# Rows on POOL's queue, one route for both tiles, and the second norm's scale and shift by feature, in a two-layer trunk

## The chip, the cores and the metric

The kernel runs on one core of a Trainium2 chip. The metric is the device time of one execution in microseconds; the kernel before takes 2118.0 us, the median of three runs (2116.41 to 2120.69). PE is the matmul engine, DVE, ACT and POOL are the vector, scalar and GpSimd engines, and SP issues most of the transfers.

## The reference

Two layers act on 256 latent and 256 context rows of 1024 features; layer 1 updates the latent rows alone. A layer normalizes and modulates its rows, projects them, mixes them in three branches (Hyena, gated DeltaNet or GDN, latent attention), merges these under gates, and projects with `w_out`. Then comes a second norm and a mixture of 16 experts, two for each row. What the change touches is this:

```python
def gdn_output(o, z, lp):
    on = o * lax.rsqrt(jnp.mean(o * o, axis=-1, keepdims=True) + EPS) * lp['gdn_norm_g']
    y = on * jax.nn.silu(z).reshape(B, L, H, DV)
    return y.reshape(B, L, H * DV) @ lp['gdn_out']

# in a layer; mix is the merged branches times w_out
x = x + gt1 * mix
h2 = rms_norm(x, lp['norm2_g']) * (1.0 + sc2) + sh2
x = x + gt2 * moe_ffn(h2, router_w, router_b, lp)

def moe_ffn(h, router_w, router_b, lp):
    scores = jax.nn.sigmoid(h @ router_w)
    sel = scores + router_b
    # the group of four experts with the largest sum of its two best, then the two best in it
    ...
    for e in range(N_EXPERTS):
        he = jax.nn.silu(h @ lp['moe_w1'][e]) * (h @ lp['moe_w3'][e])
        out = out + gate[:, e:e + 1] * (he @ lp['moe_w2'][e])
```

## The kernel before, in words

Rows are held in tiles of 128: four in layer 0 (two of x, two of ctx), two in layer 1. SBUF is an arena of 47 pages of 128x1024 floats, handed out and taken back as the program goes; `M.get(2)` takes one page. The program is written out by a planner: each piece of work is an item with loads, a preparation, matmuls and a post, and generators (`start`, with a `yield` wherever another piece may be put in) run beside the items. The planner keeps an estimated clock for each engine and queue (`enter`, lines 225 to 320, where a gather counts 2500 ns beyond its transfer) and with it decides what is written next; after that every engine works through its own instructions in the order written. Every operation goes through one helper, so all rows of the profile show line 210, and tiles are told apart by their names.

`wout_items` (line 1772) makes the output projection. An item takes a block of 128 rows of `w_out`, which ACT and DVE split into a high and a low part (the CAST is ACT's, the subtraction DVE's), and then three matmuls for each half of each tile. Layer 0 has two groups of two tiles, layer 1 one group. At item `ROWK` (0 in layer 0, 2 in layer 1) it calls `rows()`, which takes pages and issues the loads on ACT's queue: the residual rows (`load_x`, `load_x2`), norm2_g, and the modulation rows (the gate `g1`, `A2` and `B2`) out of `modd`; POOL turns A2 into (1 + sc2) times norm2_g. There is a set of modulation rows for x and, in layer 0, one for ctx. The post of a tile multiplies by the gate row, adds to the residual (two pairs of DVE operations), and starts `ffn_in`.

`ffn_in` squares on ACT, transposes on PE, multiplies by `rwA` for the router scores, computes r = 1/rms on DVE (t_rf...), then h = x r on DVE, times A2 and plus B2 on POOL, and stores h to `h2d`. `route` runs in two parts: all tiles but the last, then the last. Each part goes from the scores (t_rsc) through group sums (t_rpr) to the choice t_rA, counts positions with matmuls by triangular and all-ones matrices (t_uSb, t_onesb), and gathers the first expert's or set's rows by matmuls of h with a selection matrix. For the other experts the rows come by indirect transfers of POOL from `h2d`; `expert_in` transposes them and `expert_split` brings them from PSUM. Layer 0 then runs 16 experts (`moe_items`) of 12 weight loads, layer 1 12 sets of packed rows (`moe_sets`) with 192 loads in all, issued by SP as pages come free.

`gdn_pair` ends with the GDN output of two heads: a square and a product by 1/rms per sequence, both 128x512 on POOL, before PE's transposes.

Of the kernel before, what the change touches and what calls it, by code (L numbers as in the profile page):

```python
# [22 lines left out]
AF = mybir.ActivationFunctionType  # L23
# [7 lines left out]
L = 2  # L31
# [195 lines left out]
class Plan:  # L227
# [26 lines left out]
    def enter(self, eng, op, a, k):  # L254
# [17 lines left out]
        if "dma" in op:  # L272
# [6 lines left out]
            end = self.dma[eng] + (2500 if far else 0)  # L279
# [79 lines left out]
class Trunk:  # L359
# [334 lines left out]
    def load_x(self, l):  # L694
        xs = []
        for t in range(4):
            b = self.M.get(2)
            src = (self.a["x"][0] if t < 2 else self.a["ctx"][0])[128 * (t % 2):128 * (t % 2) + 128] if l == 0 else self.xd[128 * t:128 * t + 128]
            self.nc.scalar.dma_start(out=b.f(), in_=src)
            xs.append(b)  # L700
        return xs
# [227 lines left out]
    def gdn_pair(self, l, hp):  # L929
# [84 lines left out]
        for i, s in enumerate(seqs):  # L1014
            sq = M.get()
            g_.tensor_tensor(sq.f(), oacc[s].f(), oacc[s].f(), op=OP.mult)
            v.tensor_reduce(ss[:, 4 * i:4 * i + 4], sq.f().rearrange("p (u x) -> p u x", u=4), axis=AX.X, op=OP.add)
            sq.free()
# [5 lines left out]
        for i, s in enumerate(seqs):  # L1024
            o3 = oacc[s].f().rearrange("p (u x) -> p u x", u=4)
            g_.tensor_tensor(o3, o3, ro[:, 4 * i:4 * i + 4].unsqueeze(2).to_broadcast([128, 4, 128]), op=OP.mult)
# [743 lines left out]
    def mod_row(self, l, vec, i):  # L1770
        return self.row(self.modd[l][i:i + 1, D * vec:D * vec + D])

    def wout_items(self, l, need):
# [18 lines left out]

        def item(g, k, lag):
# [44 lines left out]
            return Item(*(([(2, ld)], prep) if k < 8 else ()), mm=mm, post=post, name=f"woutt{g}{k}", need=need, grow=22 if g == 0 and k == ROWK[l] else 0)  # L1838
# [48 lines left out]
    def router_weights(self, l, mds):  # L1887
# [9 lines left out]
        A3 = A.rearrange("p (k i) -> p k i", i=2)  # L1897
        nc.vector.tensor_tensor(self.rwA, self.rw[:, :, None, :].to_broadcast([128, 8, 2, 16]), A3.unsqueeze(3).to_broadcast([128, 8, 2, 16]), op=OP.mult)
# [11 lines left out]
    def route(self, l):  # L1910
# [17 lines left out]
        yield f"ffn{k - 2}"  # L1928
# [4 lines left out]
        for a, z in ((0, k - 1), (k - 1, k)):  # L1933
# [10 lines left out]
            v.tensor_reduce(S(gs, 4), p6, axis=AX.X, op=OP.max)  # L1944
            bc = lambda y: y.unsqueeze(2).to_broadcast([128, n, 4])
# [38 lines left out]
            if a == 0:  # L1984
                yield f"ffn{k - 1}"
# [81 lines left out]

    def expert_split(self, l, e, bs):
        if l == L - 1:
            x = self.M.get(2)  # L2070
            for q, copy in enumerate((self.nc.scalar.copy, self.nc.vector.tensor_copy)):
                copy(x.f(512, 512 * q), bs[q])
                self.unbank(bs[q])
            self.xT[e] = x
            return
        hi, lo = self.M.get(2, r=True), self.M.get(2, r=True)
        for q in range(2):
            self.split(hi.r(512, 512 * q), lo.r(512, 512 * q), bs[q])
            self.unbank(bs[q])
        self.xT[e] = (hi, lo)  # L2080
# [403 lines left out]
    def overflow_part(self, l, e, j):  # L2484
# [83 lines left out]
```

## Time and profile before

| | |
|---|---|
| median of three runs | 2118.0 us (2116.41 to 2120.69) |
| profiled execution | 2112.58 us, its span 2110.9 us |
| PE busy | 1853.4 us, 88% |
| DVE, ACT, POOL busy | 1296.4 (61%), 855.6 (41%), 338.4 us (16%) |
| transfers | 402.67 MB, mean 191 GB/s |
| mean granted clock of PE | 0.94 |

The durations below are those of the one profiled execution. A row of a timeline is a run of like instructions on one engine: its start, its time, the operation with what it writes and reads, and a count; in brackets stands how long the engine was idle before, and what released it. Rows named SPq, ACTq or POOLq are issues of transfers on that engine's queue. PEclk is the granted clock of PE as a share of full speed.

### The profile page before, as it was taken

What the parts mean: (1) busy time and instruction counts of PE and PEld (TensorE: products, weight loads), DVE (VectorE), ACT (ScalarE), POOL (GpSimd) and SP (SyncE); (2) the same over time, 40 slices, a digit from 0 to 9 for tenths busy, and PEclk for the clock granted to TensorE, in tenths of its full rate; (3) what the DMA queues carried; (4) which work ended last, traced back from release to release, by engine and by line L of the source; (5) the groups of instructions that cost most, each with busy time, mean ns of one, the idle gap of its engine ahead of it and who ended that gap; (6) DMA issues with size and microseconds to landing.
All of it is one profiled execution on the core that took longest, in us unless ns stands there. A gap on an engine that the chain in (4) does not pass through costs nothing. (4 is left out here: it accounts for less than half of the span.)

```text
span 2110.9 us, 32623 instructions
## 1 busy us (share of the span) xinstructions
PE 1853.4 (88%) x12413; PEld 1368.1 (65%) x12414; DVE 1296.4 (61%) x2775; ACT 855.6 (41%) x1477; POOL 338.4 (16%) x318
## 2 busy tenths in 40 slices
PE   5899989999999998699999289977999966899993
PEld 1776777777768776588888176966778855333330
DVE  2667666655576567899999567675777846111113
ACT  3342423344434423388887344523455421011101
POOL 1211221000123004311100211111012203100002
PEclk8999999999999999899999699988999986999996
DMA  9727111402362456699994839223324458699961
GB/s 332 249 82 214 56 40 52 124 21 81 120 180 59 120 189 248 230 373 384 378 383 177 276 137 291 67 43 94 80 80 132 132 174 333 225 394 390 383 239 69
DMA packets 295617, 402.67 MB, mean 191 GB/s; under 512 B 43941, under 2 KB 185771, under 8 KB 295449
## 3 DMA queue, kind: packets, MB, share of 16 engines
q1 hardware_dynamic: 271512, 360.38, 50.9%
q0 software_dynamic: 11040, 19.81, 2.8%
q10 hardware_dynamic: 12896, 20.28, 2.7%
q8 instruction: 100, 1.64, 0.3%
q14 instruction: 69, 0.56, 0.1%
HBM read 393.52 MB, written 23.20 MB: 197 GB/s over the span
## 5 line engine op out<-in xcount | busy, mean ns | idle before, releaser
L210 PE MATMUL bank<-pg,pg 128*128 128x512 f32 (+7 forms) x10732 | 1663.8, 390 | 77.0 <-ACT pg L210 48.0
L210 PEld LDWEIGHTS bank<-pg,pg 128*128 128x128 f32 (+5 forms) x10732 | 1212.9, 167 | 476.8 <-issue 199.2
L210 DVE TENSOR_TENSOR pg<-pg,pg 128x1024 fp32r<-128x1024 f32 (+14 forms) x697 | 603.2, 897 | 169.3 <-ACT pg L210 158.8
L210 ACT CAST pg<-pg 128x1024 fp32r<-128x1024 f32 (+3 forms) x460 | 427.9, 965 | 235.0 <-DVE pg L210 157.8
L210 ACT COPY pg<-bank 128x512 f32<-128x512 f32 (+5 forms) x414 | 171.0, 444 | 346.0 <-PE bank L210 301.7
L210 PE MATMUL bank<-cst,pg 128*128 128x128 f32 (+3 forms) x935 | 144.7, 292 | 103.8 <-DVE pg L210 49.7
L210 PEld LDWEIGHTS bank<-cst,pg 128*128 128x128 f32 (+1 forms) x935 | 117.8, 159 | 156.7 <-issue 54.1
L210 POOL TENSOR_TENSOR pg<-pg,pg 128x512 f32<-128x512 f32 (+3 forms) x77 | 131.6, 1714 | 446.2 <-DVE pg L210 274.1
L210 ACT ACTIVATE pg<-bank 128x512 f32<-128x512 f32 (+1 forms) x116 | 60.7, 534 | 197.2 <-PE bank L210 175.0
L210 DVE SCALAR_TENSOR_TENSOR pg<-bank,vec,pg 128x510 f32<-128x510 f32 (+3 forms) x112 | 73.5, 657 | 56.1 <-ACT pg L210 54.2
L210 DVE SCALAR_TENSOR_TENSOR pg<-pg,bank 128x512 f32<-128x512 f32 (+1 forms) x92 | 54.2, 601 | 84.6 <-ACT pg L210 72.3
L210 ACT ACTIVATE pg<-pg 128x512 f32<-128x512 f32 (+4 forms) x71 | 49.0, 698 | 138.7 <-DVE pg L210 123.4
L210 POOL DMA_INDIRECT yd<-pg,t_vi x28 | 29.0, 1037 | 467.6 <-ACT pg L210 232.0
L210 POOL TENSOR_TENSOR pg<-pg 128x512 f32<-128x512 f32 (+1 forms) x18 | 20.4, 1142 | 454.5 <-ACT pg L210 306.9
L210 DVE TENSOR_TENSOR pg<-bank,pg 128x512 fp32r<-128x512 f32 (+4 forms) x120 | 69.1, 596 | 30.7 <-ACT pg L210 23.5
L210 DVE COPY pg<-bank 128x512 f32<-128x512 f32 x24 | 16.6, 692 | 112.1 <-PE bank L210 90.8
L210 DVE TENSOR_TENSOR pg<-pg,bank 128x512 f32<-128x512 f32 (+1 forms) x44 | 27.0, 613 | 79.8 <-PE bank L210 77.0
L210 ACT CAST pg<-bank 128x512 fp32r<-128x512 f32 (+1 forms) x72 | 35.7, 517 | 96.9 <-PE bank L210 72.7
L210 ACT ACTIVATE pg<-bank,t_amx,t_asq 128x512 f32<-128x512 f32 (+1 forms) x48 | 33.9, 707 | 75.1 <-DVE t_amx L210 75.1
L210 ACT ACTIVATE pg<-bank,vec 128x512 f32<-128x512 f32 (+3 forms) x64 | 41.3, 646 | 53.6 <-PE bank L210 47.3
L210 PE MATMUL bank<-pg,sc 128*32 128x512 f32 x384 | 53.9, 634 | 0.7 <-DMA pg<-in_w_ada_dram 0.7
L210 DVE TENSOR_REDUCE pg<-pg 128x128 f32<-128x1024 f32 (+15 forms) x128 | 43.1, 336 | 4.4
(250 smaller groups left out, 785.0 us busy)
## 6 DMA issues: line engine op xcount, KB each, us to landing
pg<-in_moe_w_dram SPq DMA_DIRECT2D x384, 512.0 KB
pg<-in_w_in_dram SPq DMA_DIRECT2D x120, 512.0 KB
pg<-in_w_ada_dram SPq DMA_DIRECT2D x96, 512.0 KB
pg<-in_w_out_dram SPq DMA_DIRECT2D x24, 512.0 KB
pg<-modd ACTq DMA_DIRECT2D x12, 512.0 KB
pg<-yd SPq DMA_DIRECT2D x12, 512.0 KB
pg<-in_mla_w_uq_dram SPq DMA_DIRECT2D x16, 288.0 KB
pg<-gcd POOLq DMA_DIRECT2D x16, 256.0 KB, 3.8
```

The lines of the kernel that those rows point to most:

```text
L210: return f(*a, **k)
```

## The change

1. `rows()` issues its loads on POOL's queue. In layer 1 the rows norm2_g, A2 and B2 are no longer loaded, so three loads remain of six.
2. The square of the GDN output is made by ACT, the product by DVE.
3. In layer 1 `route` takes both tiles in one part, and waits for both; in both layers it yields at three more places.
4. In layer 1 h is x r alone (half by ACT, half by DVE). Scale and shift are applied where the transposed rows, with features on partitions, leave PSUM: `modulate` takes eight pieces of 128x128, four on ACT and four on DVE, each with two per-partition operands.
5. The planner counts 3800 ns for a gather, and reserves 6 pages for `rows()` in layer 1.

```diff
@@ -276,7 +276,7 @@
-            end = self.dma[eng] + (2500 if far else 0)
+            end = self.dma[eng] + (3800 if far else 0)
@@ -1013,7 +1013,7 @@
-            g_.tensor_tensor(sq.f(), oacc[s].f(), oacc[s].f(), op=OP.mult)
+            nc.scalar.activation(sq.f(), oacc[s].f(), AF.Square)
...
-            g_.tensor_tensor(o3, o3, ro[:, 4 * i:4 * i + 4].unsqueeze(2).to_broadcast([128, 4, 128]), op=OP.mult)
+            v.tensor_tensor(o3, o3, ro[:, 4 * i:4 * i + 4].unsqueeze(2).to_broadcast([128, 4, 128]), op=OP.mult)
@@ -1778,16 +1778,19 @@
-            self.xt = self.load_x(l)[:tiles] if l == 0 else self.load_x2(l, tiles)
+            q = nc.gpsimd
+            self.xt = self.load_x(l, q)[:tiles] if l == 0 else self.load_x2(l, tiles, q)
             self.g1, self.mod2, self.h2 = {}, {}, {}
-            g2 = self.row(self.a["norm2_g"][l:l + 1])
             for i in range(tiles // 2):
-                self.g1[i] = self.mod_row(l, 2, i)
-                A2 = self.mod_row(l, 4, i)
-                self.mod2[i] = (A2, self.mod_row(l, 3, i))
-                nc.gpsimd.tensor_scalar(A2.f(), A2.f(), 1.0, None, op0=OP.add)
-                nc.gpsimd.tensor_tensor(A2.f(), A2.f(), g2.f(), op=OP.mult)
-            g2.free()
+                self.g1[i] = self.mod_row(l, 2, i, q)
+            if l < L - 1:
+                g2 = self.row(self.a["norm2_g"][l:l + 1], q)
+                for i in range(tiles // 2):
+                    A2 = self.mod_row(l, 4, i, q)
+                    self.mod2[i] = (A2, self.mod_row(l, 3, i, q))
+                    nc.gpsimd.tensor_scalar(A2.f(), A2.f(), 1.0, None, op0=OP.add)
+                    nc.gpsimd.tensor_tensor(A2.f(), A2.f(), g2.f(), op=OP.mult)
+                g2.free()
@@ -1866,13 +1869,18 @@
-        A2, B2 = self.mod2[i]
-        v.tensor_scalar(h.f(), x.f(), r, None, op0=OP.mult)
-        g_.tensor_tensor(h.f(), h.f(), A2.f(), op=OP.mult)
-        g_.tensor_tensor(h.f(), h.f(), B2.f(), op=OP.add)
...
+        if l < L - 1:
...
+        else:
+
+            nc.scalar.activation(h.f(512), x.f(512), AF.Copy, scale=r)
+            v.tensor_scalar(h.f(512, 512), x.f(512, 512), r, None, op0=OP.mult)
@@ -1925,12 +1935,13 @@
-        yield f"ffn{k - 2}"
+        parts = ((0, k - 1), (k - 1, k)) if l < L - 1 else ((0, k),)
+        yield f"ffn{parts[0][1] - 1}"
...
-        for a, z in ((0, k - 1), (k - 1, k)):
+        for a, z in parts:
@@ -2065,12 +2079,22 @@
+    def modulate(self, x, b, chunks, scalar):
+
+        for k in chunks:
+            o, i, A2, B2 = x.f(128, 128 * k), b[:, 128 * (k % 4):128 * (k % 4) + 128], self.A2c[k], self.B2c[k]
+            if scalar:
+                self.nc.scalar.activation(o, i, AF.Identity, bias=B2, scale=A2)
+            else:
+                self.nc.vector.tensor_scalar(o, i, A2, B2, op0=OP.mult, op1=OP.add)
+
     def expert_split(self, l, e, bs):
         if l == L - 1:
             x = self.M.get(2)
-            for q, copy in enumerate((self.nc.scalar.copy, self.nc.vector.tensor_copy)):
-                copy(x.f(512, 512 * q), bs[q])
-                self.unbank(bs[q])
+            self.modulate(x, bs[0], range(4), True)
+            self.modulate(x, bs[1], range(4, 8), False)
```

Three places show how the order of instructions moves. The first is ACT in layer 1, from the end of the gates to the casts of w_out, with what each instruction waits for; xd are the residual rows, modd the modulation rows, and the last row is the square of the second norm. Before:

```order
L210 CAST pg_1813_15043<-pg_1670_13302 128x256 [waits DVE_49,Activation_49]
L210 DMA pg_1825_15081<-xd 128x1024 [waits DMAHW6_49,PE_49]
L210 DMA pg_1826_15083<-xd 128x1024 [waits DMAHW0_49,Pool_49]
L210 DMA pg_1827_15085<-in_norm_g_dram 128x1024 [waits DMAHW2_49,PE_49]
L210 DMA pg_1828_15087<-modd_78 128x1024 [waits DMAHW4_49,PE_49]
L210 DMA pg_1829_15089<-modd_78 128x1024 [waits DMAHW6_49,PE_49]
L210 DMA pg_1830_15091<-modd_78 128x1024 [waits DMAHW0_49,PE_49]
L210 CAST pg_1832_15109<-pg_1796_14890 128x1024 [waits PE_49]
L210 CAST pg_1834_15119<-pg_1797_14892 128x1024 [waits DMAHW3_49,Activation_49]
L210 CAST pg_1836_15123<-pg_1798_14894 128x1024 [waits Activation_49]
L210 CAST pg_1838_15127<-pg_1799_14896 128x1024 [waits DMAHW5_49,Activation_49]
L210 ACTIVATE pg_1852_15206,t_rf0a<-pg_1825_15081 128x512 [waits DVE_49,PE_49]
```

Now:

```order
L210 CAST pg_1815_15045<-pg_1672_13304 128x256 [waits DVE_49,Activation_49]
L210 CAST pg_1833_15107<-pg_1798_14892 128x1024 [waits DMAHW7_49,PE_49]
L210 CAST pg_1835_15111<-pg_1799_14894 128x1024 [waits DMAHW0_49,Activation_49]
L210 CAST pg_1837_15121<-pg_1800_14896 128x1024 [waits DMAHW1_49]
L210 CAST pg_1839_15125<-pg_1801_14898 128x1024 [waits DMAHW2_49]
L210 ACTIVATE pg_1853_15204,t_rf0a<-pg_1827_15083 128x512 [waits DMASW2_49,DVE_49,PE_49]
```

The six issues are gone from ACT, and the first cast of w_out follows the last cast of the gates. Three of the issues stand on POOL's queue instead, behind its last product of the GDN stage (t_beta) and ahead of the stores of h and the clearing of the gather pages:

```order
L210 TENSOR_TENSOR pg_1780_14599<-pg_1634_12731,t_beta 128x2x128 [waits PE_49]
L210 DMA pg_1827_15083<-xd 128x1024 [waits DMAHW7_49,PE_49]
L210 DMA pg_1828_15085<-xd 128x1024 [waits DVE_49,Activation_49]
L210 DMA pg_1829_15087<-modd_78 128x1024 [waits PE_49]
L210 DMA h2d_84<-pg_1855_15206 128x1024 [waits DVE_49,Activation_49]
L210 MEMSET pg_1866_15284 128x1024 [waits PE_49]
L210 MEMSET pg_1867_15285 128x1024 [waits PE_49]
L210 MEMSET pg_1868_15286 128x1024 [waits DMAHW6_49,DMAHW1_49,PE_49]
L210 DMA h2d_84<-pg_1873_15296 128x1024 [waits DMASW6_49,DVE_49,Activation_49]
```

The square and the product of the GDN output, and the arithmetic on A2 and h, which stood between t_beta and the stores, are no longer on POOL.

The second place is DVE in layer 1 around the choice of tile 0. Before, from the choice within the group to the post of tile 1 (the 128x512 rows that read banks):

```order
L210 COPY_PREDICATED t_rmk<-t_rgm,t_rsel 128x16
L210 MAX t_rtop<-t_rmk 128x8
L210 MAX_INDEX t_rix<-t_rtop,t_rmk 128x8
L210 CAST t_rxf<-t_rix 128x2
L210 TENSOR_TENSOR t_ro_6300<-cst_72,t_rxf 128x16 x2
L210 TENSOR_TENSOR t_rA<-t_ro_6300 128x16
L210 SCALAR_TENSOR_TENSOR pg_1864_15299<-bank_66,pg_1828_15087 128x512
L210 TENSOR_TENSOR pg_1826_15083<-pg_1826_15083,pg_1864_15299 128x512
L210 SCALAR_TENSOR_TENSOR pg_1864_15299<-bank_68,pg_1828_15087 128x512
```

Now, from tile 0's h (half of it) and its scores:

```order
L210 TENSOR_SCALAR pg_1855_15206<-pg_1827_15083,t_rf0b 128x512
L210 SCALAR_TENSOR_TENSOR score<-bank_64,t_rf0b,t_cB 128x16
L210 SCALAR_TENSOR_TENSOR pg_1864_15277<-bank_65,pg_1829_15087 128x512
L210 TENSOR_TENSOR pg_1828_15085<-pg_1828_15085,pg_1864_15277 128x512
L210 SCALAR_TENSOR_TENSOR pg_1864_15277<-bank_66,pg_1829_15087 128x512
L210 TENSOR_TENSOR pg_1828_15085<-pg_1828_15085,pg_1864_15277 128x512
L210 TENSOR_TENSOR t_rf1a<-t_rf1a 128x1
L210 TENSOR_SCALAR t_rf1a<-t_rf1a 128x1
L210 TENSOR_SCALAR t_rf1b<-t_rf1a 128x1
```

The post of tile 1 stands directly behind the scores of tile 0, and the whole route comes later, for both tiles. The third place is PE in layer 1 behind the last matmuls of w_out. Before:

```order
L210 LDWEIGHTS t_uSb
L210 MATMUL bank_63<-t_rA,t_uSb 128x16
L210 MATMUL bank_64<-cst_71,pg_1826_15083 128x128 x4
L210 MATMUL bank_65<-cst_71,pg_1826_15083 128x128 x4
L210 MATMUL bank_70<-pg_1857_15255,pg_1854_15208 128x128 x2
L210 MATMUL bank_67<-t_rwA,pg_1872_15322 128x16 x8
L210 MATMUL bank_70<-pg_1857_15255,pg_1854_15208 128x128 x2
L210 MATMUL bank_69<-pg_1857_15255,pg_1854_15208 128x128 x4
L210 LDWEIGHTS t_uSb
L210 MATMUL bank_63<-t_rA,t_uSb 128x16
L210 LDWEIGHTS t_onesb
L210 MATMUL bank_63<-t_rA,t_onesb 128x16
```

Now:

```order
L210 MATMUL bank_68<-cst_71,pg_1828_15085 128x128 x4
L210 MATMUL bank_67<-cst_71,pg_1828_15085 128x128 x4
L210 MATMUL bank_69<-t_rwA,pg_1872_15295 128x16 x8
L210 LDWEIGHTS t_uSb
L210 MATMUL bank_70<-t_rA,t_uSb 128x32
L210 LDWEIGHTS t_onesb
L210 MATMUL bank_70<-t_rA,t_onesb 128x16
L210 MATMUL bank_63<-pg_1875_15334,pg_1855_15206 128x128
L210 MATMUL bank_63<-pg_1875_15334,pg_1873_15296 128x128
```

Tile 1's transposes and its router matmuls (t_rwA) stand ahead of the one position matmul (t_uSb), and the gather matmuls of both tiles behind it, in turns.

## Rows read from the trace of the kernel before

**Rows 1.** Windows, expert stage of layer 1: us, busy by engine, PEclk, DMA share, GB/s.
```profile
1950.00:2020.00 70.00, 70.00 (x636) 22.95 (x640) 8.27 (x12) 7.65 (x13) 4.03 (x4) 1.00 1.03 386
```

**Rows 2.** Timeline of SP: start us, us, engine, line, operation, count.
```profile
877.83 250.08 SPq L210 DMA_DIRECT2D pg<-in_moe_w_dram  x164
...
1723.63 308.58 SPq L210 DMA_DIRECT2D pg<-in_moe_w_dram  x192
```

**Rows 3.** Timeline of PE at the end of both expert stages.
```profile
1154.36 8.46 PE L210 MATMUL bank<-pg,pg 128*128 128x512 f32 x36
...
2061.78 12.22 PE L210 MATMUL bank<-pg,pg 128*32 128x512 f32 x112
```

**Rows 4.** Timeline of ACT, layer 0; brackets: idle before, and what ended it.
```profile
789.73 6.99 ACTq L210 DMA_DIRECT2D pg<-modd  x6
796.76 8.82 ACT L210 CAST pg<-pg 128x1024 fp32r<-128x1024 f32 x9 [8.91 <-DMA pg<-in_norm_g_dram]
```

**Rows 5.** Timeline of PE, layer 0, from the GDN output to the route.
```profile
755.23 0.59 PE L210 MATMUL bank<-cst,pg 128*128 128x128 f32 x2 [3.80 <-POOL pg L210]
...
797.86 0.79 PE L210 MATMUL bank<-pg,pg 128*128 128x512 f32 x1 [5.67 <-ACT pg L210]
799.12 14.28 PE L210 MATMUL bank<-pg,pg 128*128 128x512 f32 x53 [0.47 <-DVE pg L210]
...
854.44 0.20 PE L210 MATMUL bank<-t_rA,t_uSb 128*128 128x48 bf16 x1 [8.20 <-DVE t_rA L210]
```

**Rows 6.** Timeline of ACT, layer 1, before the casts of w_out.
```profile
1737.27 8.13 ACTq L210 DMA_DIRECT2D pg<-modd  x3
1745.44 3.89 ACT L210 CAST pg<-pg 128x1024 fp32r<-128x1024 f32 x4 [9.24 <-DMA pg<-xd]
```

**Rows 7.** Timeline of PE, layer 1, from the GDN output to the first experts.
```profile
1713.20 1.12 PE L210 MATMUL bank<-cst,pg 128*128 128x128 f32 x4 [8.00 <-POOL pg L210]
...
1746.54 0.80 PE L210 MATMUL bank<-pg,pg 128*128 128x512 f32 x1 [11.88 <-ACT pg L210]
...
1765.96 2.97 PE L210 MATMUL bank<-pg,pg 128*128 128x512 f32 x12
...
1791.88 3.75 PE L210 MATMUL bank<-pg,pg 128*128 128x128 f32 x16 [0.98 <-DVE t_rpt L210]
...
1804.67 1.54 PE L210 MATMUL bank<-cst,pg 128*128 128x128 f32 x6 [6.06 <-DMA pg<-h2d,t_gi]
```

**Rows 8.** Windows, layer 1, the first two stretches of w_out's matmuls.
```profile
1746.50:1754.00 7.50, 7.00 (x19) 5.29 (x20) 4.63 (x4) 2.83 (x3) 2.78 (x1) 0.63 1.04 397
1754.00:1762.00 8.00, 8.00 (x37) 6.53 (x35) 2.68 (x4) 0.72 (x2) 2.40 (x1) 1.00 1.05 387
```

**Rows 9.** Timeline of DVE, layer 1, posts and route.
```profile
1758.80 0.69 DVE L210 SCALAR_TENSOR_TENSOR pg<-bank,pg 128x512 f32<-128x512 f32 x1 [7.65 <-PE bank L210]
...
1776.04 0.68 DVE L210 SCALAR_TENSOR_TENSOR pg<-bank,pg 128x512 f32<-128x512 f32 x1
...
1785.68 2.35 DVE L210 TENSOR_TENSOR t_rpr<-t_rsel 128x12 f32<-128x12 f32 x3
...
1790.46 0.17 DVE L210 TENSOR_TENSOR t_rA<-t_ro 128x16 bf16<-128x16 f32 x1
...
1795.66 0.69 DVE L210 COPY pg<-bank 128x512 f32<-128x512 f32 x1 [2.51 <-PE bank L210]
```

**Rows 10.** Timeline of POOL, layer 0 (first row) and layer 1.
```profile
801.70 3.42 POOL L210 TENSOR_SCALAR pg<-pg 128x1024 f32<-128x1024 f32 x1 [45.52 <-DMA pg<-modd]
...
1783.05 4.80 POOL L210 TENSOR_TENSOR pg<-pg,pg 128x1024 f32<-128x1024 f32 x2 [7.46 <-DVE pg L210]
...
1797.62 1.08 POOL L210 DMA_INDIRECT pg<-h2d,t_gi  x1 [8.89 <-DVE t_mxc L210]
```

**Rows 11.** Groups by form: shapes, count | busy, mean ns | idle before, releaser.
```profile
L210 POOL TENSOR_TENSOR pg<-pg 128x512 f32<-128x512 f32 x17 | 19.7, 1166 | 445.6 <-ACT pg L210 306.9 <-DVE t_osc L210 99.7 <-DVE pg L210 33.1
...
L210 ACT ACTIVATE pg<-bank,t_beta 128x128 f32<-128x128 f32 x32 | 10.2, 376 | 0.0
```

More of the change, by code (lines that the diff above doesn't have):

```diff
@@ L691, in ada_post, with load_x @@
         return post
-    def load_x(self, l):
+    def load_x(self, l, eng=None):
         xs = []
@@ L698, in load_x @@
             src = (self.a["x"][0] if t < 2 else self.a["ctx"][0])[128 * (t % 2):128 * (t % 2) + 128] if l == 0 else self.xd[128 * t:128 * t + 128]
-            self.nc.scalar.dma_start(out=b.f(), in_=src)
+            (eng or self.nc.scalar).dma_start(out=b.f(), in_=src)
             xs.append(b)
@@ L1768, in row, with mod_row @@
         return p
-    def mod_row(self, l, vec, i):
-        return self.row(self.modd[l][i:i + 1, D * vec:D * vec + D])
+    def mod_row(self, l, vec, i, eng=None):
+        return self.row(self.modd[l][i:i + 1, D * vec:D * vec + D], eng)
     def wout_items(self, l, need):
@@ L1837, in post, with load_x2 @@
                     self.start(f"ffn{t}", self.ffn_in(l, t, x), 4)
-            return Item(*(([(2, ld)], prep) if k < 8 else ()), mm=mm, post=post, name=f"woutt{g}{k}", need=need, grow=22 if g == 0 and k == ROWK[l] else 0)
+            return Item(*(([(2, ld)], prep) if k < 8 else ()), mm=mm, post=post, name=f"woutt{g}{k}", need=need, grow=(22, 6)[l] if g == 0 and k == ROWK[l] else 0)
         lags = [0] * (len(groups) - 1) + [SKEW[l]]
         return [item(g, k, lags[g]) for g in range(len(groups)) for k in range(8 + lags[g] * (len(groups[g]) - 1))]
-    def load_x2(self, l, tiles):
+    def load_x2(self, l, tiles, eng):
         xs = []
@@ L1845, in load_x2 @@
             b = self.M.get(2)
-            self.nc.scalar.dma_start(out=b.f(), in_=self.xd[128 * t:128 * t + 128])
+            eng.dma_start(out=b.f(), in_=self.xd[128 * t:128 * t + 128])
             xs.append(b)
@@ L1868, in ffn_in @@
         self.rsqrt(r, ss[:, 0:1], tmp)
-        A2, B2 = self.mod2[i]
-        v.tensor_scalar(h.f(), x.f(), r, None, op0=OP.mult)
-        g_.tensor_tensor(h.f(), h.f(), A2.f(), op=OP.mult)
-        g_.tensor_tensor(h.f(), h.f(), B2.f(), op=OP.add)
-        if t % 2 == 1:
-            A2.free()
-            B2.free()
+        if l < L - 1:
+            A2, B2 = self.mod2[i]
+            v.tensor_scalar(h.f(), x.f(), r, None, op0=OP.mult)
+            g_.tensor_tensor(h.f(), h.f(), A2.f(), op=OP.mult)
+            g_.tensor_tensor(h.f(), h.f(), B2.f(), op=OP.add)
+            if t % 2 == 1:
+                A2.free()
+                B2.free()
+        else:
+            nc.scalar.activation(h.f(512), x.f(512), AF.Copy, scale=r)
+            v.tensor_scalar(h.f(512, 512), x.f(512, 512), r, None, op0=OP.mult)
         g_.dma_start(out=self.h2d[l][128 * t:128 * t + 128], in_=h.f())
@@ L1897, in router_weights @@
         A3 = A.rearrange("p (k i) -> p k i", i=2)
+        self.A2c = [A3[:, k, 0:1] for k in range(8)]
+        self.B2c = [mds[1][:, k % 4, 1, k // 4, 0:1] for k in range(8)]
         nc.vector.tensor_tensor(self.rwA, self.rw[:, :, None, :].to_broadcast([128, 8, 2, 16]), A3.unsqueeze(3).to_broadcast([128, 8, 2, 16]), op=OP.mult)
@@ L1944, in route @@
             v.tensor_reduce(S(gs, 4), p6, axis=AX.X, op=OP.max)
+            yield
             bc = lambda y: y.unsqueeze(2).to_broadcast([128, n, 4])
@@ L1950, in route @@
             v.tensor_tensor(G(gm, 4, 4), G(t4, 4, 4), bc(S(mx, 1)), op=OP.is_equal)
+            yield
             v.copy_predicated(G(mk, 16, 4), S(gm, 4).bitcast(U32).unsqueeze(2).to_broadcast([128, 4 * n, 4]), s4)
@@ L1955, in route @@
                 v.max_index(out=te(ix)[:, t, :], in_max=te(top)[:, t, :], in_values=te(mk)[:, t, :])
+            yield
             v.tensor_copy(it(xf)[:, :, a:z], te(ix)[:, a:z, 0:2].rearrange("p t i -> p i t"))
@@ L1983, in route @@
                     t_.matmul(bs[j // 4][:, 128 * (j % 4):128 * (j % 4) + 128], self.h2[t].f(128, 128 * j), P0.f(128, 128 * t), start=t == 0 and j % 4 == 0, stop=t == k - 1 and j % 4 == 3)
-            if a == 0:
+            if z < k:
                 yield f"ffn{k - 1}"
@@ L2070, in expert_split @@
             x = self.M.get(2)
-            for q, copy in enumerate((self.nc.scalar.copy, self.nc.vector.tensor_copy)):
-                copy(x.f(512, 512 * q), bs[q])
-                self.unbank(bs[q])
+            self.modulate(x, bs[0], range(4), True)
+            self.modulate(x, bs[1], range(4, 8), False)
+            for b in bs:
+                self.unbank(b)
             self.xT[e] = x
@@ L2500, in overflow_part @@
                 t_.transpose(b[:, 128 * k:128 * k + 128], x.f(128, 512 * q + 128 * k), ident)
-            nc.scalar.copy(xT.f(512, 512 * q), b)
+            if l < L - 1:
+                nc.scalar.copy(xT.f(512, 512 * q), b)
+            else:
+                self.modulate(xT, b, range(4 * q, 4 * q + 4), q == 0)
             self.unbank(b)
```

## The prediction

> **What bounds the kernel now.** I read the share of busy time first (PE busy 88%), then the timeline of PE for the places where it stands still, then the engine that it waits for at each, and last the stretches in which a saving could be taken back. In the two expert stages PE does not pause: from 1950 to 2020 us it is busy 70.00 of 70.00 us, with the DMA engines at a share of 1.03 [rows 1]. The weights of the experts run well ahead, though: SyncE issues the last load of layer 0 at 877.83 + 250.08 = 1127.9 us, where PE's last expert matmuls end at 1162.8, and in layer 1 at 2032.2, where PE ends at 2074.0 [rows 2, 3]. So 35 and 42 us of lead. What is saved before an expert stage should therefore reach the end of the span. What the change touches lies in two short stretches ahead of the experts, the output projection with the second norm, and the route: about 755 to 880 us in layer 0 and 1707 to 1812 us in layer 1.
>
> There PE's waits have names. In layer 0 it waits 5.67 us for ACT until 797.86 [rows 5], and ACT itself shows why: its queue holds issues of row loads, the last six alone taking 6.99 us, and the nine casts of w_out that stand behind them begin at 796.76 [rows 4]. In layer 1 it is the same and worse: three issues of modulation rows take 8.13 us, the first cast comes at 1745.44 [rows 6], and PE has waited 11.88 us at 1746.54 [rows 7]. The issues are held up because each waits for an earlier transfer of its own lane (the DMAHW numbers in the order of ACT). After each pause the granted clock of PE is 0.63 for the next stretch (1746.5 to 1754: 19 matmuls in 7.00 us), then 1.00 (37 in 8.00, or 0.216 each) [rows 8]; 0.63 is a mixture of the two levels, 1.2 and 2.4 GHz.
>
> **The rows leave ACT's queue.** Layer 1: ACT stands idle for 9.24 us before the first cast of w_out, so the casts begin 9.2 us earlier [rows 6]. With them goes most of the pause after which the clock was low: 19 matmuls at 0.216 are 4.1 instead of 7.00 us, −2.9 [rows 8]. Together −12.1. Layer 0: the wait of 5.67 goes [rows 5], and 53 matmuls that took 14.28 take 53 × 0.216 = 11.45, −2.8 [rows 5, 8]. Together −8.5. What is late next: the casts themselves (layer 1: four in 3.9 us behind one another), which PE follows at the pace it does now. The bound on the other side is the clock's part at nothing: −5.7 and −9.2.
>
> The cover is POOL, idle in both stretches. Its issues wait for their pages alone. I estimate their releases from the ends of the instructions that the order names: x, ctx and the gate rows of layer 0 near 750 us, norm2_g, A2 and B2 near 788, layer 1's three by 1731; ACT issues the last of them now at 789.73 and 1737.27 or a little after [rows 4, 6]. If a row takes L from issue to landing, the last of layer 1 lands at 1730.7 + L and is wanted by the first post of w_out, now at 1758.80 [rows 9], then at 1746.7: free up to L = 16, and still up to 9 if it is issued as late as 1737.3. In layer 0 A2(1) is issued behind A2(0)'s arithmetic (3.42 + 2.4 us), then comes its own, then three pairs of multiplications of 4.8 and two short issues, before tile 2's h is done: 788 + 2L + 2 × 5.8 + 14.4 + 1.2 = 815.2 + 2L; it is wanted at 854.44 − 9.5 = 844.9 [rows 5, 10]: free up to L = 15. The nearest row for L is the gather, an indirect POOL transfer of 128 rows: issued 1797.62, its reader starts at 1804.67, so 7.05 us [rows 7, 10]. I take the rows at nothing.
>
> The Trainium skill speaks against this part: "SBUF — State Buffer", section "SBUF: two separate sides", says that descriptors of transfers issued from GpSimd cannot be written while VectorE runs an operation that takes both ports, and gives about 3100 ns against 620 alone. Estimated by that page, three late rows in line would land after 3 × 3.1 + 7 = 16 us, just at the edge of what is free, and the sum would be about 2094. No row here shows such a delay beside a busy DVE; the gather's 7.05 is the nearest and does not.
>
> **GDN's output leaves POOL.** PE waits for POOL at 755.23 (3.80 us) and 1713.20 (8.00) [rows 5, 7]. A POOL product of 128x512 takes 1.17 us on average, 1.04 here [rows 11]; the same size on DVE takes 0.68 or 0.69 [rows 9], and I take ACT's square at about the same less a tenth. Layer 1 has one square and one product on the chain: −0.85. Layer 0 has two sequences, so two of each: −2.0. Bounds: nothing, and the 3.80 of the wait.
>
> **Both tiles in one route (layer 1).** Tile 1's matmuls of w_out end at 1765.96 + 2.97 = 1768.93 [rows 7], but its post begins at 1776.04 [rows 9], since the route of tile 0 stands ahead of it in DVE's order. Now the post follows directly: −7.0. The one route then is as tile 1's was, which ends with t_rA at 1790.46, on operands twice as wide; such a small DVE operation takes 0.17 us [rows 9], and a few hundredths more for each of the twenty are +0.6. Inside it three additions took 2.35 us and ended 0.2 us after POOL's multiplications (1783.05 + 4.80) [rows 9, 10]; nothing of POOL stands there any more, so −2.5. Net −1.9 (bounds −2.5 and +0.6). Given back: the 16 gather matmuls of tile 0 ran while PE waited for tile 1; now they come behind the route with the other 16, which took 3.75 us [rows 7]: +3.75. The second tile's selection matrix on DVE: +0.5, an estimate of two more DVE operations of a quarter of a microsecond.
>
> **The second norm by feature (layer 1).** POOL's 4.80 us per tile go; they lay beside DVE's chain, so beyond the stall already counted they are worth nothing. The eviction of the gathered rows gets dearer: one ACT copy and one DVE copy of 128x512 (0.69) [rows 9] become four operations of 128x128 with two per-partition operands on each engine. The nearest row is ACT's 128x128 form with one pointer, 376 ns [rows 11]: 4 × 0.376 = 1.5, so +0.8 for the first set, which PE waits for. The router's operand gets the same, already inside the width above. In the eleven other sets the eviction lies beside some (2074.0 − 1804.7) / 12 = 22 us of matmuls [rows 3, 7]; without that cover 11 × 0.8 = 9 us.
> The skill prices the same operations otherwise: "ScalarE: Activation LUTs", section "What ACT_TABLE_LOAD costs", gives 186 ns + 0.833 per column, 93 more for each pointer operand and 93 less back to back; an estimate from it is 386 ns each, 1.5 us for four, and the sum stays.
>
> **What stays.** The new gather cost and the smaller page reserve in the planner leave SP's order alone, and PE's transposes of set 1 still follow 16 matmuls, so the wait of 6.06 us for the gather [rows 7] stays. In layer 0 tile 3's transposes and part of its DVE work now stand inside the route of the first three tiles, where PE waits 8.20 us for t_rA [rows 5]: between −2.7 and +2.7, the length of one post (four of 0.68); I take +1.0, since DVE works ahead of what PE waits for.
>
> **Sum.** Layer 0: −8.5 − 2.0 + 1.0 = −9.5. Layer 1: −0.85 − 12.1 − 7.0 − 1.9 + 3.75 + 0.5 + 0.8 = −16.8. Total −26.3 from the profiled execution's 2112.6, so 2086.3. That execution is 5.4 us below the median of the runs, 2118.0; I carry the 5.4 over: 2091.7, said as 2092. With all bounds on one side it is 2081 to 2102.
>
> **Rivals.**
> - *Rows land late* (0.14). POOL's transfers are held back while DVE is busy, L about 20: layer 0 loses 815.2 + 40 − 844.9 = 10.3, layer 1 4 us: 2106. For it: both stretches load DVE, and no row shows a plain row transfer of POOL's beside it. Against it: the gather's 7.05. (The page's rule above is of this kind.)
> - *Given back in the experts* (0.08). The DMA share of 1.03 says the transfers have little to spare; if the weights set the pace, I take half of the 26 as kept, midway between all and nothing: 2105. Against it: 35 and 42 us of lead, more than all that is saved.
> - *ACT was not what held PE* (0.06). If the casts would have waited for w_out's loads anyway, 8.5 + 12.1 fall out: 2112. For it: ACT's wait is put down to a DMA. Against it: that DMA is the row of xd, queued ahead.
> - *Slower: the two landings in line in layer 0* (0.06). Tile 2's h stands behind both A2 rows on POOL. From L = 28 on all of the gain is gone; at L = 30 it is 815.2 + 60 − 844.9 = 30 us more, or 2122. It needs four times the gather's time.
>
> **Chances.** The forecast has 0.66. About 0.2% (4.2 us) is what a measurement of this kernel can tell from no change. Faster by more: forecast and the first two rivals, 0.88; within: the third, 0.06; slower: the fourth, 0.06. The forecast's own range is 2081 to 2102; 8 times in 10 I expect 2078 to 2109, which takes in the late rows and half of what is given back.
>
> **What would show it.** In the changed profile: no issue of rows on ACT between the last cast of the gate stage and w_out's first; PE's waits there under 1 and 4 us, at a granted clock near 1.00; tile 1's post within 0.5 us of its last matmul; no stretched t_rpr; the gather wait again near 6 us, the experts without a pause. A post that waits for a DMA of x, xd or modd would make the first rival right; a PE wait on in_moe_w_dram the second; PE waiting for ACT as long as now the third.

## The result and the profile after

| | before | after |
|---|---|---|
| median | 2119.35 us (2116.41 to 2121.89, 4 runs) | 2094.14 us (2091.17 to 2098.43, 4 runs) |
| span of the profiled execution | 2110.9 us | 2089.5 us |
| PE busy; POOL busy | 1853.4; 338.4 us | 1847.3; 317.2 us |

The ratio is 0.9883 (0.9859 to 0.9907), or 25 us. The spans differ by 21.4 us. Matched matmul by matmul, the two profiled executions also drift by up to 3 us in stretches whose instructions the change does not touch (+1.9 us by 730 us, for one), so single stages are read below as differences within a stage.

The timeline of PE after the change, layer 0, from the GDN output on (answers to [rows 5]):

```profile
756.17 0.44 PE L210 MATMUL bank<-cst,pg 128*128 128x128 f32 x2 [1.75 <-DVE pg L210]
...
762.09 43.19 PE L210 MATMUL bank<-pg,pg 128*128 128x512 f32 x188 [0.22 <-DVE pg L210]
...
858.28 0.20 PE L210 MATMUL bank<-t_rA,t_uSb 128*128 128x48 bf16 x1 [5.10 <-DVE t_rA L210]
...
877.01 1.97 PE L210 MATMUL bank<-cst,pg 128*128 128x128 f32 x8 [5.62 <-DMA pg<-h2d,t_gi]
```

And the row of before that answers to its last one, the transposes that wait for the first gather:

```profile
878.15 1.92 PE L210 MATMUL bank<-cst,pg 128*128 128x128 f32 x8 [4.18 <-DMA pg<-h2d,t_gi]
```

The pause of 5.67 us is gone: 188 matmuls of w_out run without a stop and end at 762.09 + 43.19 = 805.3, where the last of before ended at 799.12 + 14.28 = 813.4; the granted clock is 1.00 from 789 to 805 us. The wait for the GDN output fell from 3.80 to 1.75. But t_rA of the first three tiles reaches PE at 858.28 against 854.44, 12 us lost against the matmuls, and the first gather is only 1.1 us ahead.

POOL in layer 0, the rows:

```profile
751.30 0.58 POOL L210 DMA_DIRECT2D pg<-in_x_dram  x1 [29.60 <-PE bank L210]
...
780.34 0.53 POOL L210 DMA_DIRECT2D pg<-modd  x1 [2.37 <-PE bank L210]
...
781.03 0.53 POOL L210 DMA_DIRECT2D pg<-modd  x1 [0.16 <-issue]
...
784.49 3.31 POOL L210 TENSOR_SCALAR pg<-pg 128x1024 f32<-128x1024 f32 x1 [2.93 <-DMA pg<-modd]
```

An issue takes 0.5 to 0.6 us, and POOL's arithmetic on a modulation row begins 784.49 − 780.34 = 4.2 us after the row's issue, long before it is wanted. Other rows take longer from issue to landing (medians): 8.2 us for x, 12.0 for ctx and 14.6 for the two gate rows, which are issued directly behind one another from 751.30 on; in layer 1 it is 7.8 us for xd and 9.5 for the gate row. PE and the posts wait for none of them.

PE in layer 1, from the GDN output to the end of the experts (answers to [rows 3, 7]):

```profile
1713.32 1.12 PE L210 MATMUL bank<-cst,pg 128*128 128x128 f32 x4 [7.01 <-DVE pg L210]
...
1737.03 0.79 PE L210 MATMUL bank<-pg,pg 128*128 128x512 f32 x1 [2.54 <-ACT pg L210]
...
1738.29 14.91 PE L210 MATMUL bank<-pg,pg 128*128 128x512 f32 x53 [0.47 <-DVE pg L210]
...
1756.99 3.01 PE L210 MATMUL bank<-pg,pg 128*128 128x512 f32 x12
...
1769.83 0.19 PE L210 MATMUL bank<-t_rA,t_uSb 128*128 128x32 bf16 x1 [4.96 <-DVE t_rA L210]
...
1771.11 5.34 PE L210 MATMUL bank<-pg,pg 128*128 128x128 f32 x32 [1.07 <-DVE pg L210]
...
1786.83 1.97 PE L210 MATMUL bank<-cst,pg 128*128 128x128 f32 x8 [6.71 <-DMA pg<-h2d,t_gi]
...
2043.49 12.22 PE L210 MATMUL bank<-pg,pg 128*32 128x512 f32 x112
```

Its granted clock around w_out, and the expert stage (windows, the columns of [rows 1, 8]):

```profile
1737.00:1743.00 6.00, 5.51 (x12) 4.03 (x13) 4.63 (x4) 2.81 (x3) 0.00 (x0) 0.50 1.05 391
1745.00:1753.00 8.00, 8.00 (x36) 6.50 (x35) 2.68 (x4) 0.72 (x2) 0.00 (x0) 1.00 1.05 386
1950.00:2020.00 70.00, 70.00 (x640) 22.72 (x636) 10.31 (x21) 9.83 (x21) 2.99 (x3) 1.00 1.00 377
```

Offsets to before: +0.1 us at the GDN output, −9.5 at the first w_out matmul behind the pause, −9.0 at tile 1's last ones (1756.99 against 1765.96), −17.8 at the first gather, −18.3 at the end of the experts (2043.49 + 12.22 = 2055.7 against 2074.0). The experts have no pause. ACT's first cast of w_out now follows the gate's casts in one row:

```profile
1735.62 4.19 ACT L210 CAST pg<-pg 128x256 fp32r<-128x256 f32 x5 [1.34 <-DVE pg L210]
```

DVE in layer 1 (answers to [rows 9]): tile 1's post, the route's t_rsc, t_rpr and t_rA, and the eviction with scale and shift:

```profile
1759.35 0.69 DVE L210 SCALAR_TENSOR_TENSOR pg<-bank,pg 128x512 f32<-128x512 f32 x1 [1.50 <-PE bank L210]
...
1766.13 0.18 DVE L210 TENSOR_SCALAR t_rsc<-t_rsc 128x32 f32<-128x32 f32 x1 [0.29 <-ACT t_rsc L210]
...
1766.57 0.35 DVE L210 TENSOR_TENSOR t_rpr<-t_rsel 128x24 f32<-128x24 f32 x3
...
1769.59 0.19 DVE L210 TENSOR_TENSOR t_rA<-t_ro 128x32 bf16<-128x32 f32 x1
...
1776.48 1.37 DVE L210 TENSOR_SCALAR pg<-bank,t_A2c,t_mod 128x128 f32<-128x128 f32 x4 [3.86 <-PE bank L210]
```

The post of tile 1 stands 16.7 us earlier, t_rA 20.9 us. The three additions of t_rpr take 0.35 us instead of 2.35.

### The profile page after: what moved, and what is told of

It is laid out like the page before. It is cut to its first block, busy times and chain, and to the rows that moved or that the text cites. A ratio compares the mean times of both kernels' runs of the same rounds, so it can differ in the third digit from the quotient of the medians.

```text
span 2089.5 us, 32684 instructions
## 1 busy us (share of the span) xinstructions
PE 1847.3 (88%) x12412; PEld 1365.2 (65%) x12413; DVE 1299.6 (62%) x2799; ACT 872.7 (42%) x1520; POOL 317.2 (15%) x314
## 5 line engine op out<-in xcount | busy, mean ns | idle before, releaser
L210 ACT COPY pg<-bank 64x256 f32<-64x256 f32 (+5 forms) x402 | 164.2, 441 | 285.2 <-PE bank L210 241.1
L210 POOL TENSOR_TENSOR pg<-pg,pg 128x512 f32<-128x512 f32 (+3 forms) x71 | 116.9, 1651 | 434.7 <-DVE pg L210 239.6
L210 DVE SCALAR_TENSOR_TENSOR pg<-bank,vec,pg 128x510 f32<-128x510 f32 (+3 forms) x112 | 73.5, 657 | 57.1 <-ACT pg L210 55.3
L210 POOL TENSOR_TENSOR pg<-pg 128x512 f32<-128x512 f32 (+1 forms) x13 | 16.0, 1235 | 423.3 <-ACT pg L210 375.6
L210 DVE COPY pg<-bank 128x512 f32<-128x512 f32 x12 | 8.3, 692 | 82.2 <-PE bank L210 75.3
```

Of the source, the lines that this page charges most:

```text
L210: return f(*a, **k)
```

## The experiments

All times are medians; each kernel was compared with the kernel before on its own chip (2117.5 to 2119.2 us).

**1. Rows on ACT's queue again.**
```diff
-            q = nc.gpsimd
+            q = nc.scalar
```


> The changed kernel with its row loads issued on ACT's queue again (layer 0: 11, layer 1: 3), all else kept. Theory (what held PE was the issues standing ahead of the w_out casts in ACT's queue): both pauses come back, about 10 us in layer 0 and up to 9.6 us in layer 1, so 2105 to 2114 us against 2094, and in layer 1 perhaps less, since three issues need fewer lanes than six. Rival (the casts would have waited for the loads of w_out anyway): within 3 us of 2094, and PE's wait ahead of w_out stays near 2.5 us.

Measured: 2106.33 us, ratio 0.9932 (0.9909 to 0.9954), 12 us worse than the changed kernel. ACT's issues and casts, and PE's waits for them:

```profile
795.18 3.55 ACTq L210 DMA_DIRECT2D pg<-modd  x4
...
1746.12 0.81 ACTq L210 DMA_DIRECT2D pg<-xd  x2
...
1747.03 0.39 ACTq L210 DMA_DIRECT2D pg<-modd  x1
...
1747.46 3.88 ACT L210 CAST pg<-pg 128x1024 fp32r<-128x1024 f32 x4 [1.01 <-issue]
```

```profile
799.87 0.80 PE L210 MATMUL bank<-pg,pg 128*128 128x512 f32 x1 [5.17 <-ACT pg L210]
...
1748.56 0.79 PE L210 MATMUL bank<-pg,pg 128*128 128x512 f32 x1 [3.67 <-ACT pg L210]
```

In layer 0 the pause is back (5.17 us). In layer 1 most of it is not: three issues are done in 1.3 us (1746.12 to 1747.42), the casts begin directly behind them, and PE waits 3.67 us instead of 2.54. So in layer 1 loading three rows fewer was nearly enough: from the GDN output to the first gather's reader the trace has 76.3 us here, 73.5 in the changed kernel and 91.5 before. Of the 12 us most lies in layer 0, and about 3 behind the experts (below).

**2. The rows alone, on the kernel before** (issues of `rows()` on POOL, nothing else).

> The kernel before with only the row loads moved to POOL's queue (11 and 6). Theory: ACT's pauses go in both layers, -10 and -9.6 us, and nothing of layer 0's gain is given back, since the route has no new yields: about 2099 us against 2119. Rival (in the changed kernel part of what looks like ACT's gain comes from the GDN output or from POOL's missing arithmetic): 2105 to 2112 us.

Measured: 2102.68 us, 0.992 (0.990 to 0.994), −16.5 us, nearer to the theory's 2099 than to the rival. PE's pause in layer 1:

```profile
1740.51 0.50 PE L210 MATMUL bank<-pg,pg 128*128 128x512 f32 x1 [2.54 <-ACT pg L210]
```

It falls to 2.54 us here too, with six rows on POOL. The queue or the smaller number of rows: either takes most of layer 1's pause away, and the changed kernel pays for it twice.

**3. The new yields in layer 1 only.**
```diff
+            if packed:
-            yield
+                yield
```
(at all three places; `packed` is true in layer 1)

> The changed kernel with the three new yields of the route in layer 1 only. Theory (in layer 0 the yields let tile 3's post and second norm into the route of the first three tiles, so t_rA came 10.6 us later against the matmuls than before, of which 5.7 us remained at the first gather): t_rA of layer 0 comes near 848 us instead of 858, the first gather's reader 4 to 6 us earlier, 2088 to 2091 us against 2094. Rival (the last tile's chain sets the end anyway, whatever stands in the first part): within 1.5 us of 2094.

Measured: 2086.69 us, 0.9851 (0.9834 to 0.9868), a little under the theory's 2088. PE in layer 0:

```profile
847.85 0.20 PE L210 MATMUL bank<-t_rA,t_uSb 128*128 128x48 bf16 x1 [8.22 <-DVE t_rA L210]
...
871.80 1.10 PE L210 MATMUL bank<-cst,pg 128*128 128x128 f32 x8 [1.85 <-DMA pg<-h2d,t_gi]
```

t_rA at 847.85 instead of 858.28, the first gather's reader at 871.80 instead of 877.01. The yields cost the changed kernel 5.2 us at the first gather by these traces, and 7.5 us by the two medians; the two intervals still touch (0.9868 and 0.9859), but experiments 5, 8 and 9, whose layer 0 has no new yields either, lie at 2086 to 2087 us as well. What stands ahead of t_rA in layer 0 of the changed kernel, on DVE: two subtractions of the weight split, tile 3's post, the product of tile 3's norm, and two small operations of the route, which ran for 2.47 us beside POOL's multiplications of tile 3 (from 853.12, 4.80 us) and for 0.33 us in this experiment:

```profile
843.78 2.35 DVE L210 TENSOR_TENSOR pg<-pg,pg 128x1024 fp32r<-128x1024 f32 x2
846.05 0.68 DVE L210 SCALAR_TENSOR_TENSOR pg<-bank,pg 128x512 f32<-128x512 f32 x1
...
852.28 0.75 DVE L210 TENSOR_SCALAR pg<-pg,t_rf3b 128x1024 f32<-128x1024 f32 x1
...
855.51 2.47 DVE L210 TENSOR_TENSOR t_ro<-cst,t_rxf 128x48 f32<-128x48 f32 x2
```

**4. Layer 1's route in two parts, with the yields.**
```diff
-        parts = ((0, k - 1), (k - 1, k)) if l < L - 1 else ((0, k),)
+        parts = ((0, k - 1), (k - 1, k))
```


> The changed kernel with layer 1's route in two parts again (tile 0, then tile 1), the rest kept. Theory (the route of tile 0 held back tile 1's post on DVE): the post of tile 1 comes about 4 to 7 us later, less 3.75 us of gather matmuls that leave the end: +2 to +6 us, 2096 to 2100 against 2094. Rival (what made the route shorter is POOL's multiplications being gone, and with the new yields the post slips in between the parts anyway): within 1.5 us, or faster.

Measured: 2091.79 us, 0.9869 (0.9853 to 0.9886), no slower than with one part. The theory that one part for both tiles gained in layer 1 falls; its rival named two reasons, and the next run separates them.

**5. The route as before, in both layers** (two parts, no new yields).

> The changed kernel with the route as it was before in both layers: two parts, none of the three new yields. Theory (in layer 1 it is the yields that let tile 1's post in between, so that one part or two made no difference; in layer 0 they cost 7 us): layer 0 wins 7 us, layer 1 loses 4 to 7 us since the post of tile 1 stands behind the whole route of tile 0 again: 2090 to 2096 against 2094 (and 2087 with the yields in layer 1 alone). Rival (the route of layer 1 gained by POOL's missing multiplications, not by its order): 2085 to 2089.

Measured: 2087.09 us, 0.9851 (0.9835 to 0.9868): the same as with the yields in layer 1, and the rival's time. So order did next to nothing in layer 1, although tile 1's post stands behind tile 0's route once more: from the GDN output to the first gather's reader it is 74.4 us here, 73.8 in experiment 4 and 73.5 in the changed kernel. DVE in layer 1, t_rsc, t_rpr, the cast of the indices, tile 1's post, tile 1's t_rA:

```profile
1755.44 0.17 DVE L210 TENSOR_SCALAR t_rsc<-t_rsc 128x16 f32<-128x16 f32 x1 [0.28 <-ACT t_rsc L210]
...
1755.86 0.33 DVE L210 TENSOR_TENSOR t_rpr<-t_rsel 128x12 f32<-128x12 f32 x3
...
1758.11 0.76 DVE L210 CAST t_rxf<-t_rix 128x2 f32<-128x2 uint32 x1
...
1759.30 0.68 DVE L210 SCALAR_TENSOR_TENSOR pg<-bank,pg 128x512 f32<-128x512 f32 x1
...
1769.59 0.17 DVE L210 TENSOR_TENSOR t_rA<-t_ro 128x16 bf16<-128x16 f32 x1
```

and the same operations of tile 0 before, then POOL's multiplications and clearing beside them:

```profile
1767.43 2.08 DVE L210 TENSOR_SCALAR t_rsc<-t_rsc 128x16 f32<-128x16 f32 x1 [0.28 <-ACT t_rsc L210]
...
1769.75 2.35 DVE L210 TENSOR_TENSOR t_rpr<-t_rsel 128x12 f32<-128x12 f32 x3
...
1774.03 1.58 DVE L210 CAST t_rxf<-t_rix 128x2 f32<-128x2 uint32 x1
```

```profile
1767.08 4.84 POOL L210 TENSOR_TENSOR pg<-pg,pg 128x1024 f32<-128x1024 f32 x2 [10.61 <-DVE pg L210]
...
1772.84 2.75 POOL L210 MEMSET pg<- 128x1024 f32 x3
```

The route of tile 0 takes 1759.30 − 1755.44 = 3.9 us from t_rsc to the post of tile 1, instead of 1776.04 − 1767.43 = 8.6. In the kernel before three of its rows took 1.6 to 2.4 us each: the first two stand beside the two multiplications on POOL of tile 0, the cast beside POOL's clearing of the gather pages. With the multiplications gone the route runs free of them; the clearing remains and holds the cast of tile 0 for 0.76 us.

**6. Layer 1's second norm by rows again** (six rows on POOL's queue, POOL multiplies, plain evictions; one-part route).

> The changed kernel with the second norm of layer 1 by rows again: norm2_g, A2 and B2 loaded (on POOL's queue), A2 and B2 applied by POOL to h, plain copies of the gathered rows. Theory (POOL's 4.8 us per tile stand beside DVE's chain, which they stall by about 2.5 us; the eviction costs 0.8 less): +1 to +4 us, 2095 to 2098 against 2094. Rival (h and its store now lie on the path to the first set): +5 to +10 us. Other rival (the scale by feature costs more in the twelve evictions than it saves): faster than 2094.

Measured: 2095.52 us, 0.9897 (0.988 to 0.9913): by the medians 1.4 us, and by the ratios 3 us worse than the changed kernel, with overlapping intervals; the trace has the first gather's reader at 1791.24 against 1786.83. DVE's t_rsc and t_rpr, and POOL's products beside them:

```profile
1768.27 1.40 DVE L210 TENSOR_SCALAR t_rsc<-t_rsc 128x32 f32<-128x32 f32 x1 [0.29 <-ACT t_rsc L210]
...
1769.93 2.37 DVE L210 TENSOR_TENSOR t_rpr<-t_rsel 128x24 f32<-128x24 f32 x3
```

```profile
1757.60 5.15 POOL L210 TENSOR_TENSOR pg<-pg,pg 128x1024 f32<-128x1024 f32 x2 [10.46 <-DVE score L210]
...
1767.29 4.80 POOL L210 TENSOR_TENSOR pg<-pg,pg 128x1024 f32<-128x1024 f32 x2 [0.89 <-issue]
```

The stalls are back (1.40 and 2.37 us), once for both tiles instead of once each. Here the single route does help: it meets POOL once. From the GDN output to the first gather's reader it is 78.2 us here and 81.9 in experiment 2, the old route beside the same products on POOL (it differs in the GDN output and layer 0's yields as well). So beside these products the single route is worth 3 to 4 us, and without them under 1: the two parts of the change cover for each other.

**7. GDN output on POOL again.**
```diff
-            nc.scalar.activation(sq.f(), oacc[s].f(), AF.Square)
+            g_.tensor_tensor(sq.f(), oacc[s].f(), oacc[s].f(), op=OP.mult)
...
-            v.tensor_tensor(o3, o3, ro[:, 4 * i:4 * i + 4].unsqueeze(2).to_broadcast([128, 4, 128]), op=OP.mult)
+            g_.tensor_tensor(o3, o3, ro[:, 4 * i:4 * i + 4].unsqueeze(2).to_broadcast([128, 4, 128]), op=OP.mult)
```


> The changed kernel with the square and the product of the GDN output on POOL again. Theory (the four GDN outputs of the two layers each stand in PE's way; PE's waits for the product are 22.8 us before and 16.5 us after): +3 to +6.5 us, 2097 to 2100 against 2094. Rival (hidden behind other work, or given back by DVE being busier): within 1.5 us.

Measured: 2097.35 us, 0.9897 (0.9881 to 0.9914), about 3 us worse than the changed kernel, of the expected sign, but the two intervals overlap; PE's wait in layer 0 is 3.80 us again.

**8. Index arithmetic first** (on experiment 3: the positions, their matmuls and the first gathers written ahead of the last gather matmuls).

> The changed kernel with the new yields in layer 1 only (2086.7 us so far) and, in the last part of the route, the index arithmetic and the first gathers written ahead of the selection matrix and its matmuls for the first expert or set, instead of behind. Theory (PE waits 6.7 us in layer 1 and 1.9 in layer 0 for the first gather, which is issued only after the 32 and 16 gather matmuls): the gather goes out about 5 us earlier in layer 1 and 2 us in layer 0, and what was behind it moves up by 3.5 to 5 and 1 to 2 us: 2079 to 2083. Rival (the index arithmetic on DVE delays the selection matrix by as much as the gather gains): 2085 to 2088.

Measured: 2086.64 us, 0.9858 (0.9842 to 0.9875), no gain: the theory's 2079 to 2083 is missed. PE in layer 1, the position matmuls and the wait for the gather:

```profile
1766.32 0.35 PE L210 MATMUL bank<-pg 128*128 128x32 bf16 x4 [1.47 <-DVE pg L210]
...
1779.94 1.97 PE L210 MATMUL bank<-cst,pg 128*128 128x128 f32 x8 [4.08 <-DMA pg<-h2d,t_gi]
```

The gather is awaited 4.08 us instead of 6.79, and layer 1 gains 3 us against the matmuls before it; in layer 0 the first expert's matmuls begin 6.2 us behind the last t_rA instead of 3.5 to 4.6 (experiments 3, 5 and 9), since its selection matrix is now late. What became of layer 1's 3 us in the median is not shown.

**9. The same in layer 1 only.**

> The changed kernel with the new yields in layer 1 only, and the index arithmetic and first gathers ahead of the gather matmuls in layer 1 only. Theory (in layer 1 index-first brought the first set 3.0 us forward against the matmuls before it; in layer 0 it held the first expert up by 1.2 us): 2082 to 2085 us, against 2086.7 without it. Rival (the 3 us are given back later, at the first weights or the last rows): 2086 to 2088.

Measured: 2086.21 us, 0.9832 (0.9812 to 0.9852), the lowest ratio of all, not to be told from experiment 3, and not the theory's 2082 to 2085. The trace again has 3.0 us in layer 1. The four kernels without the new yields in layer 0 (experiments 3, 5, 8 and 9) have medians of 2086.2 to 2087.1 us and can't be told apart; the changed kernel and experiment 4, which have them, stand at 2094.1 and 2091.8.

**10. Layer 1's norm by feature alone, on the kernel before.**

> The kernel before with only layer 1's second norm by feature: three rows fewer, no arithmetic of POOL on A2 and h, modulate at the evictions; rows on ACT's queue, GDN on POOL, route in two parts without the new yields. Theory (layer 1 has two savings, the held issues of six rows and POOL's stalls of DVE in the route, and this part alone takes away nearly all of both; neither queue nor order is needed there): PE's pause ahead of w_out falls from 11.9 to about 3.7 us, the route of tile 0 on DVE from 9.1 to 4.4 us, together -13 to -17 us: 2102 to 2106 against 2119 (and layer 0 as before). Rival (the pause needs the other queue, and the route the new order): 2112 to 2117.

Measured: 2100.84 us, 0.9908 (0.9891 to 0.9925), −18 us. PE's pause and its wait for t_rA of tile 0:

```profile
1745.57 0.79 PE L210 MATMUL bank<-pg,pg 128*128 128x512 f32 x1 [3.66 <-ACT pg L210]
...
1770.62 0.17 PE L210 MATMUL bank<-t_rA,t_uSb 128*128 128x16 bf16 x1 [2.20 <-DVE t_rA L210]
```

3.66 us instead of 11.88, and t_rA is awaited for 2.20 instead of 7.24. Matched by matmuls, layer 1 gains 14 us. Of DVE's stalls in the route only the cast's is left, at 0.84 us. This one part, with neither the queue nor the order, makes most of layer 1's gain.

The planner's two numbers were not run by themselves: with 2500 ns and 22 pages the same operations come in the same order on all five engines, a few of them on exchanged buffers.

## Why the prediction was right, and where it failed

The time was right: 2092 forecast, 2094.1 measured. Between the two traces it was less close: 26.3 us forecast, 21.4 measured. The range of 2081 to 2102 isn't what its stated bounds add up to, about 2086 to 2104; 2094.1 lies in both. Point by point:

- *Rows off ACT's queue*: right in layer 0 in size (−8.5 forecast; from +0.9 us at the GDN output to −8.1 at w_out's end, −9.1). In layer 1 the −9.2 came (−9.6), but experiments 1 and 10 show that the three rows which fell away would have brought most of it on ACT's queue as well; I had put it down to the queue alone.
- *The clock*: right in layer 0, where no pause is left. In layer 1 the −2.9 did not come: a wait of 2.54 us remains, for casts that still follow those of the gates, and behind it the granted clock is 0.50, the lower of the two levels, from 1737 to 1743; the 53 matmuls take 14.91 us instead of 14.36.
- *GDN output*: −2.05 in layer 0 by PE's wait, −1.0 in layer 1 (8.00 to 7.01); 2.0 and 0.85 were forecast.
- *Both tiles in one route*: the step that failed in its cause. "Now the post follows directly: −7.0" and the route's −1.9 gave −8.9; t_rA moved by 20.9 − 9.0 = 11.9 us relative to w_out's end, more than that. But experiments 4 and 5 show that the order brings nothing once POOL's arithmetic is gone. What held tile 1's post was a route stretched by POOL, and I had counted one of its stalls (2.5 us, tile 1's) where there were five: 2.08, 2.35 and 1.58 in tile 0's route, 0.83 and 2.35 in tile 1's. The norm by feature, which I had put at "worth nothing" beyond that stall, brings the gain without the order; beside POOL's products the order brings about half of it, estimated from experiments 2 and 6.
- *Given back behind the route*: 5.05 forecast (3.75 + 0.5 + 0.8), 20.9 − 17.8 = 3.1 measured. The dearer eviction itself came as forecast: 1.37 us for DVE's four operations, 1.51 for ACT's.
- *What stays, layer 0*: the step that failed in size. "I take +1.0, since DVE works ahead of what PE waits for", bounds ±2.7: the reorder cost 5 to 7 us (experiment 3). The yields let in not only tile 3's post but its whole second norm, and two subtractions of the weight split, so t_rA stood behind all of it, and behind a stall by POOL's products of tile 3; I had bounded it by the post alone.
- *The rivals*: no post waited for a row, so the late rows did not come. The experts gave nothing back (−17.8 at the first gather, −18.3 at their end). The slower case needed landings of 28 us for the A2 rows; 4.4 was measured (the median of A2's and B2's four), and the longest of all rows was near 15, for rows not wanted for 50 us. The third rival falls with the pauses: with the rows back on ACT, layer 0's returns (experiment 1).

Layer 0 thus brought 3 to 4 us of the 9.5 forecast, layer 1 18 to 19 where 16.8 were forecast, and about 3 us more came behind the experts. The instructions there are the same, but the rows' queue shows: from the last expert matmul to the end of the span it is 36.9 us before and 36.7 in experiments 1 and 10, which all have the rows on ACT's queue, and 33.3 to 35.1 in the nine kernels that have them on POOL's. In the traces POOL's closing drain takes 11.46 us in the first three and 3.6 to 3.9 in the others; why, stays open, and the forecast had no such term. So the total came out partly by luck: a loss in layer 0 that I had not seen was nearly made up by gains in layer 1 and at the end that I had not counted.

The Trainium skill's rule ("SBUF — State Buffer", section "SBUF: two separate sides") that VectorE, in an operation on both of its ports, can starve descriptors of transfers issued by GpSimd is borne out by no row here: issues of 0.5 to 0.6 us, and landings of 4.1 to 4.4 us beside a DVE busy 6.20 of 8.00 us. The landings of 8 to 15 us come where several rows are issued one behind the other and the DMA engines stand at a share of 0.98 (748 to 756 us) and 0.96 (1724 to 1734); what made them longer no run separates. The other direction is what mattered: the Trainium skill's section "Who interferes with whom" says that where the two engines contend for their shared pair of ports, whoever comes first holds it for a whole instruction. By that the stalls of DVE end with POOL's instruction, and the trace agrees: the cast at 1774.03 ended at 1775.61, the clearing on POOL at 1775.59.

## What to carry to other kernels

When one wait hides two causes, a change that removes both looks as if each part were needed; undo the parts singly, and also do them singly on the kernel before. A place where the order may be changed (a yield) costs nothing only if what it lets in is short: look up in the new order everything that stands in between, not only the first item. And where a chain of small vector operations takes ten times its usual length, look at what GpSimd does at the same moment before reordering the chain.

## What the runs showed of the hardware

A pause of 2.5 us was followed by as low a clock as one of 11.9 us: 0.50 in the first 6 us behind it, where the kernel before had 0.63 on average over 7.5 us [rows 8]. Over the 6 us from 1731 to 1737, with that pause at their end, PE had been busy for 2.44. Not expected either was how long DVE's large operations can be held: in layer 0 of the changed kernel two subtractions of 128x1024, 1.25 us each on average in the kernel before, took 6.68 us together beside POOL's products:

```profile
820.74 6.68 DVE L210 TENSOR_TENSOR pg<-pg,pg 128x1024 fp32r<-128x1024 f32 x2
```

```profile
820.63 5.71 POOL L210 TENSOR_TENSOR pg<-pg,pg 128x1024 f32<-128x1024 f32 x2 [1.17 <-DVE pg L210]
```
